# Last stage of a hybrid decoder step: transposes ahead of the values' product, output bank taken later

## The chip, the core and the metric

The kernel runs on one core of a Trainium2 chip, as one launch. Its five engines have their own instruction queues: TensorE (PE; its weight loads, which overlap the products, are shown as PEld), VectorE (DVE), ScalarE (ACT), GpSimd (POOL) and SyncE (SP), which here issues the DMA transfers. The metric is the device time in microseconds (us) of one execution; each version is run several times and the median is compared.

## The reference

One inference step of a two-layer decoder for a prompt (512 positions) and 8 short samples (4 positions each). The first layer is a Mamba-2 mixer, the second a dilated-window attention mixer over a shared K/V. Cut to the second layer, which the change is about:

```
def dilated_mixer(h, attend, biases, g_norm, w_in, w_out):
    u = rmsnorm(h, g_norm) @ w_in
    q = u[..., :Q_WIDTH]  # 3 dilation groups x 8 heads x 128
    gate = u[..., Q_WIDTH:]
    for g in range(3):
        o, lse = attend(q[:, :, g], biases[g], DILATIONS[g], WINDOWS[g] // DILATIONS[g])
    w = softmax(stack(lses)); o = sum(w * outs)
    y = o * silu(gate)
    return y @ w_out
# attend: scores = q k^T * scale + bias, masked to the window; p = softmax(scores); o = p v
```

For the prompt the keys are the 512 positions themselves; for the samples they are 640 kept rows of a cache and the 4 new rows. The final RMSNorm follows.

## The kernel before

All matmuls are in fp32; the large projections are split into a high and a low part (names `whi`, `wlo`, `yh`, `yl`) and are written as three products for each 128-row block. Everything up to the shared K/V lies ahead of the last stage, which runs from about 600 us to the end and which alone the change touches.

The last stage does two things at once. A **filler** (`pair_filler`, L1118, and then `out_proj`, L1421) yields one matmul of a projection at a time: first the query and gate projections by pairs of tiles (outputs `pa` and `pb`, from `bq` and `whi`/`wlo`), then the output projection (from `yh`/`yl` and `wo`). The **attention units** are generators that stop between their parts:

- `attend(h, n)` (L1241): one head h and one block n of 128 prompt queries. Part 1 computes the scores (`sp`, L1254 to L1258: eight products with 32 columns of weights each, one for each quarter of the queries and each of two dilation groups, then one with 128) and the exponentials. Part 2 transposes the weights of the softmax (`ptp`, L1272 to L1276: two or three transposes against the identity) and copies them to `pt`. Part 3 is the values' product (`pv`, L1281 to L1287): first one or two products with the full 128x128 weights, then four with 32 columns and w = 32(n + 1) rows of weights (32, 64, 96 or 128 for n = 0 to 3); ScalarE scales it to `on`. Part 4 transposes `on` into the head's output bank `op` (L1291) and, after the fourth block, copies it out.
- `sample(h, q)` (L1307): one head and four samples. Part 1 loads the cached keys (`kc`, two transfers of 640 KB, L1316), computes the scores (`s`, with 32 columns of weights, L1318 to L1322) and asks for the cached values (`vc`, two transfers, L1337). Part 2 asks for the new values (`vn`, L1340) and transposes (`w`, six transposes). Part 3 is the values' product (`so`, L1350 to L1357): 20 products with 128 rows and 32 columns of weights, then four with 4 rows and 32 columns.

`units` (L1483) puts the units in a row: for each of heads 0 to 6 attend 0, sample 0, attend 1, attend 2, sample 1, attend 3; then for head 7 sample 0, attend 2, sample 1, attend 3, `combine`, attend 0, attend 1. The loop at L1492 goes through them step by step. In step u it advances the units u - 4 (its output transpose), u - 3 (its values' product) and u - 2 (its transposes), in this order, then starts unit u (its scores), and then takes 24 matmuls (20 from step 44 on) from the filler. So each unit is spread over five steps, and TensorE's instructions stand in program order. `kc` and `vc` have two buffers each, both of which one sample unit uses: a unit's `kc` can only be loaded when the scores of the sample unit before have been computed, and its `vc` when that unit's `so` is done. All of these transfers are issued by SP, one after the other in the order in which they stand there.

PSUM has eight banks: three for the projections and five (`pss`, L160) for everything in the attention, so that `op`, `sp`, `ptp`, `pv`, `s1`, `s2`, `w1`, `w2` and `so` share five. The head's `op` is taken by its first unit at the very start of part 1, four steps before its first output transpose.

A scheduler that works with estimated times orders the instructions of ACT, DVE and SP as they come out of the program, so a shift of work can also change their order.

Of the kernel before, what the change touches and what calls it, by code (L numbers as in the profile page):

```python
# [124 lines left out]
def tile_yoco_step(  # L125
# [10 lines left out]
    def pin(ins):  # L136
        if pinned[0]:
            tc.keep_in_program_order(ins)
# [3 lines left out]
    def mm(*a, **k):  # L142
        pin(nc.tensor.matmul(*a, **k))  # L143

    def transpose(*a):
        pin(nc.tensor.transpose(*a))  # L146
# [13 lines left out]
    def pss(name, shape=(128, 512)):  # L160
        return psum.tile(list(shape), F32, name=name, tag="ss", bufs=5)
# [616 lines left out]
    def run(n):  # L778
        for _ in range(n):
            if next(fill, 0) == 0:  # L780
                return
# [275 lines left out]
    qp_t, kv_t = {}, {}  # L1057

    def fetch_kv(h):
        kv_t[h] = kv = half("kv")  # L1060
        dma(kv[:, 0, :], kvd[h, :, 0:T])
        dma(kv[:, 1, 0:SEQ], kvd[h, :, T:T + SEQ])
        for n in range(4):
            dma(kv[32 * n:32 * n + 32, 2, 0:SEQ].rearrange("p (r d) -> p r d", r=4),
                dap(kvd, h * 128 * (T + SEQ) + T + 128 * n, [[T + SEQ, 32], [32 * (T + SEQ), 4], [1, 128]]))
# [153 lines left out]
    def y_split(h, c0, c1):  # L1219
        i, k = h // 4, h % 4  # L1220
        if y_h[i] is None:
            late_split.append((h, c0, c1))
            return
        split2(y_h[i][:, k, c0:c1], y_l[i][:, k, c0:c1], y_t[i][:, k, c0:c1])
# [7 lines left out]
    def bias_tile(h):  # L1232
        bt = wk.tile([128, 512], F32, name="bt", bufs=2)
        for r in range(4):
            dma(bt[32 * r:32 * r + 32, 0:256].rearrange("p (a c) -> p a c", c=32),
                dap(bvd, h * 32 * VN + r * 8 * 63 + 31, [[VN - 1, 32], [63, 8], [1, 32]]))
            dma(bt[32 * r:32 * r + 32, 256:512].rearrange("p (a c) -> p a c", a=2),
                dap(bvd, h * 32 * VN + V0N + 31, [[VN - 1, 32], [V1N, 2], [1, 128]]))
        return bt

    def attend(h, n):  # L1241
        if h not in op_t:
            op_t[h] = pss("op")
        op, bt, qp = op_t[h], bt_t[h], [qp_t[h, g] for g in range(3)]
        kv = kv_t[h]
        kt = kv[:, 0, :]
        vb, vr = (kv[:, i, 0:SEQ].rearrange("p (n d) -> p n d", n=4) for i in (1, 2))
        ktr = kt[:, 0:SEQ].rearrange("p (n r i) -> p r n i", n=4, r=4)
        bt12 = bt[:, 256:512].rearrange("p (a c) -> p a c", a=2)
        w = 32 * (n + 1)  # L1250
        g0 = 128 if n == 0 else 256
        sp = pss("sp")
        k0 = max(0, n - 1) * 128
        for g in range(2):  # L1254
            for r in range(4):
                mm(sp[32 * r:32 * r + 32, g0 + w * g:g0 + w * g + w],
                   qp[1 + g][:, 128 * n + 32 * r:128 * n + 32 * r + 32], ktr[:, r, 0:n + 1, :], start=True, stop=True)
        mm(sp[:, 0:g0], qp[0][:, 128 * n:128 * n + 128], kt[:, k0:128 * n + 128], start=True, stop=True)  # L1258
        s_ = wk.tile([128, 512], F32, name="s", bufs=3)
        mx = wk.tile([128, 4], F32, name="mx", bufs=4)  # L1260
        s12 = s_[:, g0:g0 + 2 * w].rearrange("p (a c) -> p a c", a=2)
        nc.vector.tensor_tensor_reduce(out=s12, in0=sp[:, g0:g0 + 2 * w].rearrange("p (a c) -> p a c", a=2),
                                       in1=bt12[:, :, 128 - w:128], scale=1.0, scalar=-3e38,
                                       op0=ALU.add, op1=ALU.max, accum_out=mx[:, 1:2])
        nc.vector.tensor_tensor_reduce(out=s_[:, 0:g0], in0=sp[:, 0:g0], in1=bt[:, 256 - g0:256], scale=1.0,
                                       scalar=-3e38, op0=ALU.add, op1=ALU.max, accum_out=mx[:, 0:1])
        nc.vector.tensor_scalar(mx[:, 2:3], mx[:, 0:1], mx[:, 1:2], -1.0, op0=ALU.max, op1=ALU.mult)
        nc.scalar.activation(s_[:, 0:g0 + 2 * w], s_[:, 0:g0 + 2 * w], AF.Exp, bias=mx[:, 2:3], accum_out=mx[:, 3:4])
        nc.vector.tensor_tensor(s12[:, 0, :], s12[:, 0, :], s12[:, 1, :], op=ALU.add)
        nc.vector.reciprocal(mx[:, 3:4], mx[:, 3:4])  # L1270
        yield
        tp = pss("ptp", (128, 3, 128))  # L1272
        nk = g0 // 128
        for i in range(nk):
            transpose(tp[:, i, :], s_[:, 128 * i:128 * i + 128], ident)
        transpose(tp[0:w, 2, :], s_[:, g0:g0 + w], ident)  # L1276
        pt = wk.tile([128, 3, 128], F32, name="pt", bufs=2)
        nc.scalar.copy(pt[:, 0:nk, :], tp[:, 0:nk, :])
        nc.scalar.copy(pt[0:w, 2, :], tp[0:w, 2, :])
        yield  # L1280
        pv = pss("pv")[:, 0:128]  # L1281
        for i in range(nk):
            b = n - nk + 1 + i
            mm(pv, pt[:, i, :], vb[:, b, :], start=i == 0, stop=False, skip_group_check=True)
        for r in range(4):
            mm(pv[32 * r:32 * r + 32, :], pt[0:w, 2, 32 * r:32 * r + 32], vr[0:w, r, :],
               start=False, stop=True, skip_group_check=True)  # L1287
        on = wk.tile([128, 128], F32, name="on", bufs=1)
        nc.scalar.activation(on, pv, AF.Copy, scale=mx[:, 3:4])
        yield  # L1290
        transpose(op[:, 128 * n:128 * n + 128], on, ident)  # L1291
        op_n[h] = op_n.get(h, 0) + 1
        yt = y_t[h // 4][:, h % 4, :]
        if h == 7 and op_n[h] % 2 == 0:
            c0 = HA if n > 1 else 0
            assert len(gated) == 2
            nc.vector.scalar_tensor_tensor(yt[:, c0:c0 + HA], op[:, c0:c0 + HA], 0.5, yt[:, c0:c0 + HA], op0=ALU.mult, op1=ALU.mult)
            y_split(h, c0, c0 + HA)
        elif h < 7 and op_n[h] == 4:
            nc.vector.tensor_copy(yt[:, 0:SEQ], op)  # L1300
            att_done.add(h)
# [107 lines left out]
    op_t, op_n, bt_t, late_smp = {}, {}, {}, []  # L1409
# [66 lines left out]
    def run(n):  # L1476
        m = min(n, ahead[0]) if n > OCN else 0
        ahead[0] -= m
        for _ in range(n - m):
            if next(fill, 0) == 0:  # L1480
                return

    units = [(f, (h, i)) for h in range(ATH - 1) for f, i in  # L1483
             ((attend, 0), (sample, 0), (attend, 1), (attend, 2), (sample, 1), (attend, 3))]
    units += [(sample, (7, 0)), (attend, (7, 2)), (sample, (7, 1)), (attend, (7, 3)), (combine, ()), (attend, (7, 0)), (attend, (7, 1))]
    fill = filler()
    fetch_kv(0)
# [4 lines left out]
    for u in range(len(units) + LA + 2):  # L1492
        i = u - LA
        if u == len(units) - 3 + SKIP:
            ahead[0] = ATH * OCN
        for j in (i - 2, i - 1, i):
            if 0 <= j < len(units):
                next(live[j], 0)
        if u < len(units):
            f, a = units[u]  # L1500
            if f is attend and a[0] not in bt_t:
                bt_t[a[0]] = bias_tile(a[0])
            if f is attend and a[1] == 2 and 0 < a[0] < ATH - 1:
                fetch_kv(a[0] + 1)
            live.append(f(*a))
            next(live[u])
        run(FILL[u >= SLOW])
# [97 lines left out]
```

## Time and profile before

| what | us |
|---|---|
| median of 3 runs (lowest, highest) | 964.43 (963.14, 966.48) |
| the profiled execution, device time | 964.79 |
| its span, from the first to the last instruction | 963.0 |
| TensorE busy (share of the span) | 932.9 (97%) |
| VectorE busy | 682.2 (71%) |
| ScalarE busy | 482.1 (50%) |

The device time is 1.8 us longer than the span that the trace shows. A matmul's record lasts longer than the time by which it holds up the next, since matmuls overlap; so what a group of them costs is read from the start of its first record to the start of the next group's first record, not from busy time. In the rows, a shape such as 128\*32 is rows times columns of the weights, and 128x272 that of the moving operand. One fp32 matmul leaves two records, a transpose one.

### The profile page before, as it was taken

How to read it: one execution, taken by the hardware profiler on the slowest of the kernel's cores; microseconds unless marked ns; L12 is line 12 of the kernel's file. 1: busy time of each engine (PE TensorE's matmuls, PEld its weight loads, DVE VectorE, ACT ScalarE, POOL GpSimd, SP SyncE). 2: the span in 40 equal slices, each digit the busy share in tenths (PEclk: the TensorE clock that was granted, in tenths of full speed). 3: DMA queues.
4: the chain of work that ended last, by engine and by line, in shares of the span. 5: the costliest groups of instructions: out<-in, count | busy, mean ns of one | idle time of the engine just before them, and what ended most of it. 6: DMA issues, size and time to landing. Idle time of an engine off the chain costs nothing.

```text
span 963.0 us, 21807 instructions
## 1 busy us (share of the span) xinstructions
PE 932.9 (97%) x8645; PEld 847.5 (88%) x8645; DVE 682.2 (71%) x1435; ACT 482.1 (50%) x1057; POOL 200.5 (21%) x295
## 2 busy tenths in 40 slices
PE   7999998999999998999999999999999999989996
PEld 5999987889788888999999999888888888868896
DVE  6687979998998798555597347767667766757532
ACT  5558745654645654322354214555555555555542
POOL 3232545544544532111010000000000000000021
PEclk9999999899999999999999999999999999989898
DMA  7252355255366432545386556775876876844411
GB/s 259 83 157 74 120 201 190 78 166 180 130 194 205 160 114 95 154 139 194 117 272 188 197 180 188 257 251 181 271 234 197 266 264 208 276 163 158 143 45 50
DMA packets 75934, 168.49 MB, mean 175 GB/s; under 512 B 19446, under 2 KB 37192, under 8 KB 75320
## 3 DMA queue, kind: packets, MB, share of 16 engines
q1 hardware_dynamic: 71880, 154.91, 49.0%
q10 hardware_dynamic: 2880, 9.44, 2.5%
q0 software_dynamic: 1072, 2.74, 1.1%
q8 instruction: 68, 1.11, 0.5%
q14 instruction: 34, 0.28, 0.1%
HBM read 141.14 MB, written 25.93 MB: 173 GB/s over the span
## 4 chain that ended last, share of the span: by engine, by line
PE 88%; DVE 5%; DMA 3%; ACT 1%; POOL 1%; issue 1%; DVEq 0%; SPq 0%; ACTq 0%
PE pa L143 34%; PE pb L143 30%; PE sp L143 3%; PE so L143 3%; PE pv L143 2%; PE s L143 2%; PE yd L143 1%; PE ptp L146 1%; PE w L146 1%; PE csp L143 1%; PE yo L143 1%; DMA m<-aed 1%; PE xp L146 1%; DMA kc<-ck 1%; PE yos L143 1%; DVE vl L758 1%
## 5 line engine op out<-in xcount | busy, mean ns | idle before, releaser
L199 ACT ACTIVATE whi<-wraw 128x1024 fp32r<-128x1024 f32 x72 | 76.2, 1058 | 99.6 <-PE pb L143 66.2
L200 DVE TENSOR_TENSOR wlo<-wraw,whi 128x1024 fp32r<-128x1024 f32 x71 | 88.9, 1252 | 50.5 <-ACT whi L199 50.5
L143 PE MATMUL pa<-bq,whi 128*128 128x272 f32 x512 | 103.1, 297 | 0.0
L143 PE MATMUL pa<-xh,whi 128*128 128x256 f32 (+1 forms) x320 | 92.7, 293 | 3.3 <-ACT xh L365 3.3
L143 PE MATMUL pb<-xh,whi 128*128 128x288 f32 (+1 forms) x304 | 90.4, 299 | 3.9 <-ACT cb L331 3.9
L143 PE MATMUL pb<-xl,whi 128*128 128x288 f32 (+1 forms) x304 | 91.2, 302 | 0.9 <-DVE xl L368 0.8
L143 PE MATMUL pa<-xl,whi 128*128 128x256 f32 (+1 forms) x320 | 90.8, 287 | 0.9 <-DVE xl L368 0.8
L143 PE MATMUL pb<-xh,wlo 128*128 128x288 f32 (+1 forms) x304 | 87.4, 299 | 0.0
L143 PE MATMUL pa<-xh,wlo 128*128 128x256 f32 (+1 forms) x320 | 85.0, 283 | 0.0
L143 PEld LDWEIGHTS pa<-bq,whi 128*128 128x128 f32 x512 | 81.9, 190 | 0.9
L143 PE MATMUL pb<-bq,whi 128*128 128x272 f32 x384 | 79.9, 302 | 0.3 <-DVE kv L1100 0.2
L143 PE MATMUL pa<-bq,wlo 128*128 128x272 f32 x256 | 74.2, 290 | 0.0
L529 DVE SCALAR_TENSOR_TENSOR co<-cb,cvp,co 128x568 f32<-128x568 f32 x72 | 66.6, 925 | 1.2 <-ACT co L527 0.2
L143 PEld LDWEIGHTS pa<-xh,whi 128*128 128x128 f32 x320 | 60.7, 190 | 6.2 <-ACT xh L365 3.7
L143 PEld LDWEIGHTS pb<-bq,whi 128*128 128x128 f32 x384 | 62.5, 194 | 1.7 <-DVE qpad L1091 0.7
L143 PEld LDWEIGHTS pa<-xl,whi 128*128 128x128 f32 x320 | 60.6, 189 | 3.4 <-DVE xl L368 1.4
L143 PEld LDWEIGHTS pb<-xl,whi 128*128 128x128 f32 x304 | 57.8, 190 | 6.5 <-issue 4.4
L143 PEld LDWEIGHTS pb<-xh,whi 128*128 128x128 f32 x304 | 58.0, 191 | 5.0 <-ACT cb L331 4.1
L1332 POOL COPY lse<-mxs 128x1 f32<-128x1 f32 x16 | 3.8, 236 | 273.3 <-DVE mxs L1330 273.3
L143 PEld LDWEIGHTS pa<-xh,wlo 128*128 128x128 f32 x320 | 58.0, 188 | 1.3 <-issue 0.9
L1158 ACT ACTIVATE whi<-wraw 128x512 fp32r<-128x512 f32 x64 | 40.2, 628 | 37.4 <-PE pa L143 17.1
L143 PEld LDWEIGHTS pb<-xh,wlo 128*128 128x128 f32 x304 | 56.6, 190 | 2.2 <-issue 2.2
(378 smaller groups left out, 2786.8 us busy)
## 6 DMA issues: line engine op xcount, KB each, us to landing
wraw<-w_in SPq DMA_DIRECT2D x40, 512.0 KB
kc<-ck SPq DMA_DIRECT2D x32, 640.0 KB
vc<-cv SPq DMA_DIRECT2D x32, 640.0 KB
wraw<-wb SPq DMA_DIRECT2D x32, 512.0 KB
s<-s SPq DMA_DIRECT2D x16, 512.0 KB
m<-aed SPq DMA_DIRECT2D x16, 512.0 KB
ssmS<-s ACTq DMA_DIRECT2D x16, 512.0 KB
wraw<-w_out SPq DMA_DIRECT2D x16, 512.0 KB
```

The source lines that it names most:

```text
L143: pin(nc.tensor.matmul(*a, **k))
L146: pin(nc.tensor.transpose(*a))
L199: a = nc.scalar.activation(hi, raw, AF.Copy)
L200: b = lo_eng.tensor_tensor(lo, raw, f32(hi), op=ALU.subtract)
L529: nc.vector.scalar_tensor_tensor(o, cb[:, k:k + n], cvp[:, ti, k:k + 1], o, op0=ALU.mult, op1=ALU.add)
L758: nc.vector.scalar_tensor_tensor(v_l[g][:, i, :], v_t[g][:, i, :], gg, f32(v_h[g][:, i, :]), op0=ALU.mult, op1=ALU.subtract)
L1158: nc.scalar.activation(hi, src[p][j], AF.Copy)
L1332: nc.gpsimd.tensor_copy(lse[:, i16:i16 + 1], mx[:, 2:3])
```

## The change

Two edits. The loop now advances unit u - 4, then u - 2, then u - 3: within a step the transposes (`ptp` or `w`) stand right behind the output transpose and ahead of the values' product (`pv` or `so`), which now stands right ahead of the new unit's scores. And a head takes its output bank `op` when its first output transpose is issued, four steps later than before.

```
@@ attend
     def attend(h, n):
-        if h not in op_t:
-            op_t[h] = pss("op")
-        op, bt, qp = op_t[h], bt_t[h], [qp_t[h, g] for g in range(3)]
+        bt, qp = bt_t[h], [qp_t[h, g] for g in range(3)]
...
         on = wk.tile([128, 128], F32, name="on", bufs=1)
         nc.scalar.activation(on, pv, AF.Copy, scale=mx[:, 3:4])
         yield
+        if h not in op_t:
+            op_t[h] = pss("op")
+        op = op_t[h]
         transpose(op[:, 128 * n:128 * n + 128], on, ident)
...
@@ the loop over the units
-        for j in (i - 2, i - 1, i):
+        for j in (i - 2, i, i - 1):
             if 0 <= j < len(units):
                 next(live[j], 0)
```

On TensorE, in a step that starts an attend unit (`sp`) and advances an attend unit's product (`pv`) and a sample unit's transposes (`w`), the difference is:

```order
 L146 MATMUL op<-ident,on 128x128
+L146 MATMUL w_7710<-ident,ss 128x128 x4
+L146 MATMUL w_7711<-ident,ss 128x128
+L146 MATMUL w_7711<-ident,ss 4x128
 L143 MATMUL pv<-kv,pt 128x128 x2
 L143 MATMUL pv<-kv,pt 32x128 x4
-L146 MATMUL w_7719<-ident,ss 128x128 x4
-L146 MATMUL w_7720<-ident,ss 128x128
-L146 MATMUL w_7720<-ident,ss 4x128
 L143 MATMUL sp<-kv,qp 32x32 x8
```

The six transposes now follow the output transpose and precede the values' product, which borders on the scores. In the next step, with a sample unit's product, it is the same with `ptp` and `so`:

```order
 L146 MATMUL op<-ident,on 128x128
+L146 MATMUL ptp<-ident,s 128x128 x3
 L143 MATMUL so<-vc,wt 32x128 x20
 L143 MATMUL so<-vn,wt 32x128 x4
-L146 MATMUL ptp<-ident,s 128x128 x3
```

The three transposes moved from behind the product to ahead of it. On SP the order of the transfers stays as it was, but for three places; the one that lies between steps 42 and 44 (sample units of head 7, `kc` and `vc` of the text above; `wraw` are weights of the filler) stood before as

```order
L1237 DMA bt_10908<-bvd_92 32x2x128
L190 DMA wraw_10937<-wb 128x1024
L1337 DMA vc_10832<-cv 128x1280
L1337 DMA vc_10834<-cv 128x1280
L1340 DMA vn_10979<-vnd_97 4x4x128
L1316 DMA kc_10995<-ck 128x1280
L1316 DMA kc_10997<-ck 128x1280
```

and stands now (its lines are one higher there) as

```order
L1237 DMA bt_10908<-bvd_92 32x2x128
L190 DMA wraw_10936<-wb 128x1024
L1317 DMA kc_10994<-ck 128x1280
L1338 DMA vc_10832<-cv 128x1280
L1338 DMA vc_10834<-cv 128x1280
L1341 DMA vn_10969<-vnd_97 4x4x128
L1317 DMA kc_10996<-ck 128x1280
```

The first of the two `kc` transfers for the sample unit of step 44 moved ahead of the `vc` transfers of the unit before; the second stayed behind them. The other two places are early ones, where a bias transfer and a weight transfer pass ahead of a `vc`. In the last steps the transposes of attend 0 of head 7 (`ptp`) move ahead of the products of `combine` (`oc`), and ACT and DVE take the two casts of the output weights (L199, L200) some instructions earlier.

## Rows read from the trace of the kernel before

**Rows 1.** The first lines of the profile's page: the span, and busy time, share of the span and instructions of each engine.

```profile
span 963.0 us, 21807 instructions
PE 932.9 (97%) x8645; PEld 847.5 (88%) x8645; DVE 682.2 (71%) x1435; ACT 482.1 (50%) x1057; POOL 200.5 (21%) x295
```

**Rows 2.** Busy time by stretches of 10 us in the last stage: stretch, its length, busy time and instructions of PE, PEld, DVE, ACT, POOL, then the granted TensorE clock (1.00 is 2.4 GHz, 0.50 is 1.2 GHz), the share of the DMA engines' time, GB/s.

```profile
700.00:710.00 10.00, 10.00 (x136) 8.68 (x135) 6.44 (x20) 5.96 (x15) 0.00 (x0) 1.00 0.64 204
...
860.00:870.00 10.00, 9.69 (x109) 7.68 (x110) 3.83 (x13) 4.39 (x9) 0.18 (x1) 0.67 0.12 17
```

**Rows 3.** Who waited for whom, PE's matmuls alone, from 600 us to the end: total, times, longest.

```profile
PE s L143 <- DMA kc<-ck: 2.6, 2, 2.2
PE pa L143 <- ACT yh L1214: 2.3, 1, 2.3
```

**Rows 4.** Timeline of PE in a step with `op`, `pv`, `w` and `sp`: start, duration to the end of the last of the row's records, engine, line, what, number of records. The last row is the filler's first matmul.

```profile
702.33 0.27 PE L146 MATMUL op<-ident,on 128*128 128x128 f32 x1
702.44 0.97 PE L143 MATMUL pv<-kv,pt 128*128 128x128 f32 x12
703.34 0.87 PE L146 MATMUL w<-ident,ss 128*128 128x128 f32 x6
704.14 0.75 PE L143 MATMUL sp<-kv,qp 128*32 128x32 f32 x18
704.65 0.49 PE L143 MATMUL pb<-bq,whi 128*128 128x272 f32 x2
```

**Rows 5.** The same for the next step, with `op`, `so`, `ptp` and `s`, and its filler's first matmul.

```profile
707.73 0.27 PE L146 MATMUL op<-ident,on 128*128 128x128 f32 x1
707.93 1.30 PE L143 MATMUL so<-vc,wt 128*32 128x128 f32 x40
709.16 0.42 PE L143 MATMUL so<-vn,wt 4*32 4x128 f32 x8
709.51 0.55 PE L146 MATMUL ptp<-ident,s 128*128 128x128 f32 x3
709.99 1.28 PE L143 MATMUL s<-kc,qpad 128*32 128x512 f32 x16
711.24 0.52 PE L143 MATMUL pa<-bq,whi 128*128 128x272 f32 x2
```

**Rows 6.** The same in step 46, where the transposes `w` are followed by another full-width transpose (`lp`, of `combine`).

```profile
873.74 0.87 PE L146 MATMUL w<-ident,ss 128*128 128x128 f32 x6
874.45 0.27 PE L146 MATMUL lp<-ident,lse 128*16 128x128 f32 x1
```

**Rows 7.** Who waited for whom, PE's weight loads alone, 602 to 850 us: total, times, longest ("issue": no releaser is seen).

```profile
PEld ptp L146 <- issue: 3.4, 17, 0.2
...
PEld w L146 <- issue: 2.8, 14, 0.2
PEld ptp L146 <- PE so L143: 1.8, 9, 0.2
...
PEld s L143 <- DMA kc<-ck: 0.4, 1, 0.4
```

**Rows 8.** Timeline of SP: start, duration of the issue, what (x2: two transfers). The last of them is followed in time by Rows 9.

```profile
656.47 0.83 SPq L1337 DMA_DIRECT2D vc<-cv  x2
...
667.69 0.83 SPq L1316 DMA_DIRECT2D kc<-ck  x2
...
844.61 0.37 SPq L190 DMA_DIRECT2D wraw<-wb  x1
850.10 0.83 SPq L1337 DMA_DIRECT2D vc<-cv  x2
...
851.36 1.01 SPq L1316 DMA_DIRECT2D kc<-ck  x2
```

**Rows 9.** The chain of waits that ended last: start, length, what.

```profile
851.73 8.54 DMA kc<-ck
```

**Rows 10.** As Rows 2, stretches of 1 us (the last two numbers are the DMA engines' share and GB/s).

```profile
672.00:673.00 1.00, 1.00 (x19) 0.82 (x21) 0.95 (x5) 0.48 (x1) 0.00 (x0) 1.00 0.66 267
673.00:674.00 1.00, 1.00 (x40) 0.80 (x36) 0.96 (x4) 0.15 (x1) 0.00 (x0) 1.00 0.04 15
...
850.00:851.00 1.00, 1.00 (x23) 0.63 (x23) 0.00 (x1) 0.43 (x2) 0.00 (x0) 1.00 0.00 0
```

**Rows 11.** Timeline of PE: the scores `s` that the `kc` of Rows 8 belong to (674.71), and those of steps 42 and 44 with the waits in brackets, the filler's first matmul behind step 42 (845.47) and step 44 (862.64), and the first of step 45 (866.99).

```profile
674.71 1.28 PE L143 MATMUL s<-kc,qpad 128*32 128x512 f32 x16
...
843.66 1.62 PE L143 MATMUL s<-kc,qpad 128*32 128x512 f32 x12
...
845.47 0.52 PE L143 MATMUL pa<-bq,whi 128*128 128x272 f32 x2
...
855.74 0.88 PE L146 MATMUL w<-ident,ss 128*128 128x128 f32 x6
858.82 1.10 PE L143 MATMUL s<-kc,qpad 128*32 128x512 f32 x4 [2.20 <-DMA kc<-ck]
860.31 1.06 PE L143 MATMUL s<-kc,qpad 128*32 128x512 f32 x6 [0.40 <-DMA kc<-ck]
...
862.64 0.82 PE L143 MATMUL pb<-bq,whi 128*128 128x272 f32 x2
...
866.99 0.27 PE L146 MATMUL op<-ident,on 128*128 128x128 f32 x1
```

More of the change, by code (lines that the diff above doesn't have):

```diff
@@ L1241, in attend @@
     def attend(h, n):
-        if h not in op_t:
-            op_t[h] = pss("op")
-        op, bt, qp = op_t[h], bt_t[h], [qp_t[h, g] for g in range(3)]
+        bt, qp = bt_t[h], [qp_t[h, g] for g in range(3)]
         kv = kv_t[h]
@@ L1290, in attend @@
         yield
+        if h not in op_t:
+            op_t[h] = pss("op")
+        op = op_t[h]
         transpose(op[:, 128 * n:128 * n + 128], on, ident)
@@ L1495, in tile_yoco_step @@
             ahead[0] = ATH * OCN
-        for j in (i - 2, i - 1, i):
+        for j in (i - 2, i, i - 1):
             if 0 <= j < len(units):
```

## Prediction

> **What bounds the kernel now.** The page's head comes first: TensorE is busy for 932.9 of 963.0 us, 97%, the next engine for 71% [rows 1]. That is an average, so the second view is busy time by stretches in the stage that changes: in 700 to 710 us PE is busy for 10.00 of 10.00 us at the full granted clock, and DMA has a share of 0.64 [rows 2]. The third is who waits for whom: of PE's matmuls behind 600 us two wait for cached keys (2.6 us in all) and one in the tail for `yh` (2.3 us); there is none for a PSUM bank, for `pt`, `wt` or `on` [rows 3]. So up to step 43 the stage is exactly as long as PE's instruction stream, and a change of order can save only what the order itself costs inside that stream. That is read from the timeline, from start to start.
>
> **What a change of shape costs.** An `op` transpose holds up the full-width `pv` behind it by 0.11 us (702.33 to 702.44) [rows 4], but the 32-column `so` by 0.20 (707.73 to 707.93) [rows 5]: leaving the full width costs 0.09. A second pair agrees: six `w` transposes take 0.80 until `sp` starts [rows 4], 0.71 until the full-width `lp` does [rows 6], again 0.09. Entering the full width costs as well: 0.71 for six transposes is 0.06 more than 6 x 0.11, and three `ptp` take 0.48 until `s` (709.51 to 709.99) [rows 5], which is 3 x 0.11 + 0.09 + 0.06. Narrow products before them end late, too: the four 4-row `so` take 0.35 (709.16 to 709.51), where 20 with 128 rows take 1.23, 0.0615 each [rows 5]; 0.35 less 4 x 0.0615 leaves 0.10. So a narrow shape that borders on another shape pays 0.09 to 0.10, and the entry 0.06.
>
> The weight loads show the same places: between 602 and 850 us, 17 + 14 + 9 = 40 loads of `ptp` and `w` wait for 0.2 us each, 8.0 in all, nearly one a step [rows 7].
>
> **The order of transposes and product.** A step before runs full (filler, `op`), narrow product, full (`ptp` or `w`), narrow scores, full (filler). After, the transposes lie in the first full run and the product borders on the scores. Gone are the product's exit into the transposes (0.10), the entry (0.06) and the transposes' exit into the scores (0.09): 0.25. Added is the border of product and scores. Where shapes differ (4 rows after `so`, 32 or 64 rows in `pv` of n = 0 and 1, against 128 rows) I price it as the exit between narrow and other, 0.10. Where `pv` ends with 96 or 128 rows (n = 2, 3) I take none. Bounds: 0.10 there as well, which gives back 1.3; and nothing at any border, which gains 2.8 more. I take the middle because the 4-row border is in the trace and costs, while 20 equal `so` run on without one [rows 5].
>
> The Trainium skill, page "TensorEngine Tiling (Array Packing)", Key Properties, states that changing the tiling mode, not just the tile, drains TensorE, and lists row modes of 128, 64 and 32. By that list 96 rows have no mode of their own, as I take it; were they one, the saving would be 0.7 us less. No row here shows a 96-row product beside scores.
>
> So a step saves 0.15. It has all its parts from step 3 to step 43, 41 steps: 41 x 0.15 = 6.15. Thirteen of them advance a `pv` of n = 2 or 3 (two for each of heads 0 to 6, less the last): 13 x 0.10 = 1.3. Sum 7.45 by the end of step 43. An upper bound for the 0.15 is the weight loads' whole wait of 0.2 a step, 8.2 in all; the lower is 0.09 a step, if the 0.06 was only the wait of the first transpose for its input, 3.7.
>
> **The output bank.** Nothing. PE waits for no bank [rows 3], so a bank that is taken four steps later frees nothing that anyone waits for. The last user of the bank that `op` now gets is a group of an earlier step, and the filler's 24 matmuls (704.65 to 707.73, 3.08 us) [rows 4, 5] cover its eviction. Bounds: 0 to +0.3, if an `op` transpose had to wait for the head before to be copied out, seven times at 0.04.
>
> **The transfers.** A `vc` is asked for behind a `so`, the next `kc` behind an `s`, and the scores come a fixed number of steps later. With shorter steps that distance shrinks while the transfers don't. One such path before: `vc` issued at 656.47, `kc` at 667.69 [rows 8], `s` at 674.71 [rows 11], 18.24 us. The last traffic ends soon after 672.7 (share 0.66 in 672 to 673, 0.04 in the next) [rows 10], so at most some 2 us were left, less what passes between the last packet and the signal that the matmul waits for, which no row shows. After, `so` borders on the scores, so `vc` is asked for 0.48 later within its step (the `ptp` ahead of it), and three steps are 0.55 shorter in all: 17.2. That uses up half of the margin or more; I take no new wait, and bound it by 0.1 to 0.5 at each of the dozen sample steps (third rival).
>
> Step 42 waited already: `s` to filler takes 1.81 (843.66 to 845.47) [rows 11] against 1.25 (709.99 to 711.24) [rows 5], 0.56, and its weight load 0.4 for `kc` [rows 7]. Its `kc` hangs on the scores of step 40, so what two steps save, 0.4, turns into wait there. Cover gone: 0.4 lost.
>
> **Step 44** is the one that ends late. Before, `vc` was issued at 850.10 and `kc` behind it at 851.36 [rows 8], though its buffers were free since step 42 and DMA stood at 0.00 in 850 to 851 [rows 10]: SP issues in order, and `vc` waited for `so`. The chain shows one `kc` from 851.73 on for 8.54 us [rows 9], and PE waited 2.20 and 0.40 [rows 11]. Four transfers in 8.6 us are 2.15 each. Now one `kc` goes ahead of `vc`, into the idle stretch; three are left, and the last lands 2.15 earlier, counted from `vc`. `vc` itself is asked for 0.3 later within the step (`ptp` ahead of `so`, 0.48, less the 0.15 and rounding). Steps up to there have brought 7.45 - 0.15 - 0.4 = 6.9. So the scores of step 44 go on 6.9 + 2.15 - 0.3 = 8.75 earlier. PE reaches them 6.9 to 7.05 earlier and would still wait some 2 us: the wait keeps its size but in one piece. Behind it the granted clock was 0.67 in 860 to 870 [rows 2], and I leave that as it was. Bounds of this step: 0.9 less if the three go at the 267 GB/s of a busy stretch [rows 10] (3 x 655,360 bytes in 7.4 us against 6.45), and 2.9 more if the clock stays up (second rival).
>
> Steps 45 to 48 save four times 0.14, 0.55. In the tail the products of `combine` and the casts change places around the wait of 2.3 for `yh` [rows 3]; nothing by my count, with bounds of -2.3 and +2.3, since no row says what else would come last.
>
> **Sum.** 8.75 + 0.55 = 9.3. The span goes from 963.0 to 953.7 [rows 1]; with the 1.8 outside the span 955.5. The profiled execution, at 964.79, lies 0.36 above the median of 964.43; less that, 955.1, rounded to 955.0.
>
> **Rivals.**
> 1. *Forecast*, 955.0, with its own range of 953.5 to 957.5 by the bounds of the border price and of the three transfers.
> 2. *The clock stays up at step 44.* The filler there took 4.35 for 20 matmuls (862.64 to 866.99) [rows 11]; at the pace of 3.08 for 24 it is 2.57, so 1.8 less; the rest of the scores took 2.33 (860.31 to 862.64), against 1.25 for a whole one [rows 5], 1.1 less. Together 2.9: 952. For it: the wait of one `kc` is gone. Against: the other is still waited for by some 2 us, about as long as the one that stood ahead of the fall.
> 3. *The scores catch up with the keys.* Without margin, a dozen sample steps wait 0.3 to 0.6 each, 3.6 to 5 us given back: 958 to 960. For it: 0.56 in step 42. Against: step 42 is the only one with a wait up to 850 us [rows 7].
> 4. *It doesn't do what it says.* The cost belongs to every border of groups, not to a change of shape; the same number of groups then costs the same and only step 44's transfer helps, 2.15 less 0.3: 962.6, no difference. Against: 0.11 and 0.20 behind the same `op` [rows 4, 5].
> 5. *Slower.* The scores catch up with the keys so far that PE stands as in step 44, 2.2 of wait and then 2.9 at the half clock, 5.1 a time. The place is `s` of the sample units of heads 1 to 6. Two such waits eat the 9.3, and from there it is slower; with three it is 955.1 + 15.3 = 970.4. It needs a `kc` that lands over 2 us later than I count. For it: 64% DMA share in a common stretch [rows 2]. Against: the margin loses 1.04 of about 2.
>
> **Chances.** Forecast 0.58, clock up 0.24, scores catch up 0.07, nothing done 0.05, slower 0.05, and 0.01 for the tail at its upper bound. The range reaches from 950.5 (second rival with the border free, in part) to 960.0. A measurement of this kernel tells about 0.3%, 2.9 us, from no change. The first three cases are faster by more, the fourth is within it, the fifth is slower: 0.90, 0.05, 0.05.
>
> **What would show it.** The wait of the weight loads of `w` and `ptp` gone; `op` to `w` or `ptp` 0.11; `so` to `s` about 0.10 longer than its products; step 42 waiting about 1.0 and no other sample step before it; one `kc` of step 44 in time and the other landing some 1.5 to 2 us behind PE; the filler behind it at 4.35 (forecast) or 2.6 (second rival). Wrong it would be above all if `kc` waits show in rows of steps before 42, or if `pv` ahead of the scores costs more than the transposes did.

## The result, and the profile after

The changed kernel takes 955.47 us (median of 4 runs, 954.65 to 958.56), beside 964.04 for the kernel before (4 runs, 963.14 to 966.48; the three known at the time of the prediction had a median of 964.43). The ratio is 0.9913, with a 95% interval of 0.9884 to 0.9942: faster by 0.9%. The profiled execution took 955.35, its span is 953.6 us. Forecast were 955.0 and a span of 953.7. The sum came out almost to the tenth, but not all of its terms did. Left out of the medians below are two executions in a slower state, one of e3 (1014.85 us at a granted clock of 0.84) and one of e7 (1465.11 us at 0.56).

The head of the profile's page of the changed kernel (beside [rows 1]):

```profile
span 953.6 us, 21793 instructions
PE 924.2 (97%) x8645; PEld 850.3 (89%) x8645; DVE 685.5 (72%) x1435; ACT 477.6 (50%) x1057; POOL 201.9 (21%) x295
```

TensorE (PE) has the same number of records, 8645, and the same share of the span. What changed is how much one group of them holds up the next. The timeline of PE in the same two steps as in [rows 4, 5], from the output transpose to the filler's first matmul, and ahead of them two rows of a step that advances an n = 0 block (32 rows of weights):

```profile
683.71 0.74 PE L143 MATMUL pv<-kv,pt 128*128 128x128 f32 x10
684.38 1.17 PE L143 MATMUL sp<-kv,qp 128*32 128x96 f32 x18
...
700.62 0.27 PE L146 MATMUL op<-ident,on 128*128 128x128 f32 x1
700.72 0.82 PE L146 MATMUL w<-ident,ss 128*128 128x128 f32 x6
701.38 0.96 PE L143 MATMUL pv<-kv,pt 128*128 128x128 f32 x12
702.16 0.73 PE L143 MATMUL sp<-kv,qp 128*32 128x32 f32 x18
702.64 0.49 PE L143 MATMUL pb<-bq,whi 128*128 128x272 f32 x2
...
705.74 0.27 PE L146 MATMUL op<-ident,on 128*128 128x128 f32 x1
705.85 0.49 PE L146 MATMUL ptp<-ident,s 128*128 128x128 f32 x3
706.27 1.30 PE L143 MATMUL so<-vc,wt 128*32 128x128 f32 x40
707.50 0.42 PE L143 MATMUL so<-vn,wt 4*32 4x128 f32 x8
707.85 1.28 PE L143 MATMUL s<-kc,qpad 128*32 128x512 f32 x16
...
709.10 0.39 PE L143 MATMUL pa<-bq,whi 128*128 128x272 f32 x1
```

From the first record of the step to the filler's first: with `w` and `pv` 2.02 us (700.62 to 702.64), before 2.32 [rows 4]; with `ptp` and `so` 3.36 (705.74 to 709.10), before 3.51 [rows 5]. The six `w` now hold up what follows them by 0.66 (0.80 before), the three `ptp` by 0.42 (0.48). `pv` of step 18 is of n = 2, with 96 rows of weights: it runs into `sp` after 0.78, where before it took 0.90 until `w`. For n = 0 nothing of that kind shows: 0.67 from `pv` to `sp` (683.71 to 684.38), as it took 0.67 to `w` before in the same step (684.33 to 685.00), so this border still costs, as forecast.

The weight loads that waited 0.2 us in nearly every step [rows 7] show the same. Who waited for whom, PE's weight loads alone, 602 to 848 us of the changed kernel (total in us, times, longest):

```profile
PEld s L143 <- issue: 5.8, 21, 0.3
...
PEld sp L143 <- issue: 4.6, 23, 0.2
...
PEld s L143 <- DMA kc<-ck: 1.8, 2, 1.1
```

No `ptp` and no `w` waits in this answer any more; the waits that are left are those in front of `s`, `sp` and `so`, one or two a step, and one for `kc`, of 1.8 us in two places, where it was 0.4 in one [rows 7]. These places, and step 44, in PE's timeline (beside [rows 11]):

```profile
672.83 1.53 PE L143 MATMUL s<-kc,qpad 128*32 128x512 f32 x10
...
674.97 0.52 PE L143 MATMUL pa<-bq,whi 128*128 128x272 f32 x2
...
837.07 1.80 PE L143 MATMUL s<-kc,qpad 128*32 128x512 f32 x10
...
839.48 0.52 PE L143 MATMUL pa<-bq,whi 128*128 128x272 f32 x2
...
848.71 0.82 PE L146 MATMUL w<-ident,ss 128*128 128x128 f32 x6
...
853.06 0.62 PE L143 MATMUL s<-kc,qpad 128*32 128x512 f32 x6 [1.89 <-DMA kc<-ck]
...
854.30 0.52 PE L143 MATMUL pb<-bq,whi 128*128 128x272 f32 x2
...
856.91 0.27 PE L146 MATMUL op<-ident,on 128*128 128x128 f32 x1
```

A whole `s` takes 1.25. In step 13 it takes 2.14 (672.83 to 674.97), so 0.89 of wait that was not there before [rows 11]; in step 42 it takes 2.41, so 1.16 of wait (0.56 before). In step 44 the last keys come at 853.06, 7.25 earlier than before, and the filler behind takes 2.61 for its 20 matmuls (854.30 to 856.91) instead of 4.35 [rows 11]. SP's timeline of the transfers behind these waits (beside [rows 8]):

```profile
667.22 0.83 SPq L1317 DMA_DIRECT2D kc<-ck  x2
...
839.40 0.35 SPq L1317 DMA_DIRECT2D kc<-ck  x1
844.44 0.80 SPq L1338 DMA_DIRECT2D vc<-cv  x2
...
845.97 0.33 SPq L1317 DMA_DIRECT2D kc<-ck  x1
```

The keys of step 13 are asked for only 0.47 earlier than before (667.22, 667.69 [rows 8]), while their scores come 1.88 earlier (672.83, 674.71). The first keys of step 44 are asked for at 839.40, as the scores of step 42 end, the others at 845.97 behind `vc`: one ahead, one behind, as the order showed.

The ledger of the two profiles, from step 4 on (at 620.06 in both), with what was forecast:

| term, us | forecast | measured |
|---|---|---|
| PE's stream of steps 4 to 43, waits for `kc` taken off | -7.3 | -7.63 (234.23 to 226.60) |
| new wait in step 13 | 0 to 0.1 | +0.89 |
| longer wait in step 42 | +0.4 | +0.60 |
| step 44 up to the last keys (`w` or `pv` to the second `s` row) | -1.85 | -1.11 |
| half clock behind it: rest of the scores, filler | 0 | -2.83 |
| steps 45 to 48 | -0.55 | -0.28 |
| tail from step 49 on | 0 | +0.96 |
| sum | -9.3 | -9.4 |

The forecast of the stream is 7.45 less the 0.15 of step 3. Of the 0.33 more, most comes from the steps whose `pv` has 96 or 128 rows: the one shown above saves 0.30, and 0.25 was forecast. Steps 45 to 48 save less than forecast, in part because in steps 46 and 48 a further full-width transpose (`lp`) stands among the groups; these two save 0.04 each. The rest of the scores took 2.33 before (860.31 to 862.64) and 1.24 now; with the filler that is 1.09 + 1.74 = 2.83.

### The profile page after: what moved, and what is told of

Its sections match the earlier page's. It is cut to its first block, busy times and chain, and to the rows that moved or that the text cites. A ratio compares the mean times of both kernels' runs of the same rounds, so it can differ in the third digit from the quotient of the medians.

```text
span 953.6 us, 21793 instructions
## 1 busy us (share of the span) xinstructions
PE 924.2 (97%) x8645; PEld 850.3 (89%) x8645; DVE 685.5 (72%) x1435; ACT 477.6 (50%) x1057; POOL 201.9 (21%) x295
## 3 DMA queue, kind: packets, MB, share of 16 engines
q8 instruction: 68, 1.11, 0.5%
## 4 chain that ended last, share of the span: by engine, by line
PE 87%; DVE 6%; DMA 3%; ACT 1%; POOL 1%; issue 1%; SPq 0%; DVEq 0%; ACTq 0%
PE pa L143 34%; PE pb L143 30%; PE sp L143 3%; PE so L143 3%; PE pv L143 2%; PE s L143 2%; DMA kc<-ck 1%; PE yd L143 1%; PE csp L143 1%; PE yo L143 1%; PE ptp L146 1%; PE xp L146 1%; PE w L146 1%; DVE co L529 1%; PE yos L143 1%
## 5 line engine op out<-in xcount | busy, mean ns | idle before, releaser
L199 ACT ACTIVATE whi<-wraw 128x1024 fp32r<-128x1024 f32 x72 | 76.1, 1056 | 101.5 <-PE pb L143 68.9
L200 DVE TENSOR_TENSOR wlo<-wraw,whi 128x1024 fp32r<-128x1024 f32 x71 | 90.0, 1268 | 48.1 <-ACT whi L199 47.9
```

The source lines that it names most:

```text
L199: a = nc.scalar.activation(hi, raw, AF.Copy)
L200: b = lo_eng.tensor_tensor(lo, raw, f32(hi), op=ALU.subtract)
```

## Experiments

Each ratio is to runs of the kernel before on the same chip. "Stream" is, for each, the time from step 4 to step 44 less the waits of `s` for `kc` in it, read from the starts of PE's records. Stream, waits and step 44 are those of the one execution that has a profile; it took 961.60 in e7, the longest of nine, 951.67 in e9, the longest of five, and 953.30 in e8, the shortest of five, so these do not add up to the medians.

| run | edit | median, us | ratio to before (95%) | stream | waits for `kc`, steps 13 to 42 | step 44 |
|---|---|---|---|---|---|---|
| before | | 964.04 | | 234.23 | 0.56 | 7.80 |
| after | both | 955.47 | 0.9913 (0.9884 to 0.9942) | 226.60 | 2.05 | 5.59 |
| e1_order_only | order alone | 954.71 | 0.9911 (0.9891 to 0.9931) | 226.57 | 4.44 | 6.49 |
| e2_bank_only | bank alone | 964.02 | 1.0007 (0.9994 to 1.002) | 234.22 | 0.84 | 7.54 |
| e3_product_first | third order | 963.89 | 1.0008 (0.9987 to 1.0029) | 233.94 | 0 | 8.51 |
| e5_after_keys44_pool | after, keys of 44 by GpSimd | 952.32 | 0.9889 (0.985 to 0.9929) | 226.52 | 3.33 | 2.66 |
| e6_before_keys44_pool | before, the same | 957.31 | 0.994 (0.9917 to 0.9964) | 234.24 | 0.19 | 2.95 |
| e7_after_keys44_late | after, keys of 44 behind values | 957.17 | 0.9944 (0.9924 to 0.9963) | 226.74 | 4.28 | 9.20 |
| e8_new_values_first | after, `so` reordered | 955.76 | 0.993 (0.9904 to 0.9955) | 224.68 | 2.06 | 9.13 |
| e9_keys7_pool_new_first | e8, keys of head 7 by GpSimd | 949.03 | 0.9854 (0.9831 to 0.9878) | 224.65 | 2.71 | 2.66 |

(Step 44 is from its first record to the filler's first.)

**e1_order_only and e2_bank_only.** The two edits, each alone: in e1 the changed line of the loop with `op` taken as before, in e2 the reverse.

```
-        for j in (i - 2, i - 1, i):
+        for j in (i - 2, i, i - 1):
```

> Only the order of the loop (output transpose, transposes, product, scores); the bank is taken early as before. Theory (what is saved is changes of weight-tile shape on TensorE): all of the gain, 955 to 956, step for step the times of the changed kernel (3.36 us for a step with op, ptp, so and s, 2.03 for one with op, w, pv of three or four blocks and sp). Rival (the later bank has a share): 958 to 962, with waits for a bank in front of the scores.

> Only the bank is taken later; the order is that of before. Theory: nothing, 963.5 to 965, steps as before (3.51 and 2.31 us). Rival (the bank has a share): 958 to 962.

The order has all of the gain, the bank none. Both also show a known order a second time: e2 issues the same instructions in the same order as the kernel before on every engine, and e1 the same as the changed kernel; only the banks differ. So what differs between e2 and before, or e1 and after, does not come from the order. The streams agree within 0.03 us. The clock behind step 44 does not: in e2 the filler there runs at full speed, in e1 not quite. PE's timeline of e2, and then of e1:

```profile
861.23 2.56 PE L143 MATMUL s<-kc,qpad 128*32 128x512 f32 x10 [2.23 <-DMA kc<-ck]
...
864.78 0.52 PE L143 MATMUL pb<-bq,whi 128*128 128x272 f32 x2
...
867.39 0.27 PE L146 MATMUL op<-ident,on 128*128 128x128 f32 x1
```

```profile
856.93 0.81 PE L143 MATMUL s<-kc,qpad 128*32 128x512 f32 x6 [1.95 <-DMA kc<-ck]
...
859.01 0.82 PE L143 MATMUL pb<-bq,whi 128*128 128x272 f32 x2
...
862.35 0.27 PE L146 MATMUL op<-ident,on 128*128 128x128 f32 x1
```

The filler of step 44 takes 2.61 in e2 (864.78 to 867.39) where the same instructions took 4.35 before, and 3.34 in e1 (859.01 to 862.35) where they took 2.61 after. A wait of 1.95 is followed by the half clock in e1, one of 1.89 is not in the changed kernel.

**e3_product_first.** A third order; the number of groups in a step is the same.

```
-        for j in (i - 2, i, i - 1):
+        for j in (i - 1, i - 2, i):
```

> A third order with as many groups in a step: product first, then output transpose and transposes in one row, then scores (bank taken late). The narrow product stands between two full-width runs, as before. Theory of shapes: a step costs what it cost before (3.51 us with so, 2.31 with pv of n = 2 or 3), 962 to 965 in all. Rival (the gain comes from output transpose and transposes standing in one row, or from fewer waits of the transposes for their inputs): 3.36 and 2.1 us, 955 to 957.

PE's timeline in the two steps, and then who waited, weight loads alone, 602 to 850 us:

```profile
704.23 0.96 PE L143 MATMUL pv<-kv,pt 128*128 128x128 f32 x12
705.12 0.33 PE L146 MATMUL op<-ident,on 128*128 128x128 f32 x1
705.28 0.82 PE L146 MATMUL w<-ident,ss 128*128 128x128 f32 x6
```

```profile
PEld op L146 <- issue: 3.8, 19, 0.2
```

Here `op` and `w` stand in one row, as in the changed kernel, but a narrow product stands between them and the filler. Now `op` pays the entry: it holds up `w` by 0.16 (705.12 to 705.28) instead of 0.11, and its weight load is the one that waits. The stream is back at 233.94, 0.29 below that of before, and the time is that of before. So the gain is not in having output transpose and transposes side by side; it goes with how many times a step leaves and enters the full width.

**e8_new_values_first.** In `so` the four products with 4 rows of weights go first; start and stop flags move with them.

```
-        for i in range(6):
+        for i in (5, 0, 1, 2, 3, 4):
...
```

> The changed kernel, with the four products of the new values (4 rows of weights) ahead of the 20 of the cached ones (128 rows) in so, so that so ends with the shape with which s begins. The same instructions, one change of shape fewer in a step. Theory (a change of rows costs 0.10 wherever it stands): op to s takes 2.0 us instead of 2.11 in every so step (step 3.25 instead of 3.36), 1.5 to 1.8 us in all 16 of them: 953 to 954.5. Rival (only full against narrow costs): 3.36 as it is, 955.

```profile
705.19 0.27 PE L146 MATMUL op<-ident,on 128*128 128x128 f32 x1
...
705.72 0.42 PE L143 MATMUL so<-vn,wt 4*32 4x128 f32 x8
706.07 1.30 PE L143 MATMUL so<-vc,wt 128*32 128x128 f32 x40
707.19 1.26 PE L143 MATMUL s<-kc,qpad 128*32 128x512 f32 x16
...
708.41 0.52 PE L143 MATMUL pa<-bq,whi 128*128 128x272 f32 x2
```

PE's timeline in a `so` step: 3.22 us (705.19 to 708.41) instead of 3.36, 0.14 less for one change of shape less, and the stream is 1.92 shorter. The 20 cached products hold up what follows by 1.12 (706.07 to 707.19) where they took 1.23 in front of the 4-row ones (706.27 to 707.50 above): a change of rows between narrow products costs 0.11, near the 0.10 that I took, and `s` itself ends a little sooner without it. The median did not follow. In the profile SP's order came out with both keys of step 44 behind `vc` (`vc` at 843.00, `kc` at 844.27 and 844.64), and that step took 9.13 instead of 5.59.

**e5_after_keys44_pool, e6_before_keys44_pool, e7_after_keys44_late.** The place of step 44's keys, in both orders.

```
-            dma(kc[jp], ck[h, q, :, 2 * jp:2 * jp + 2, :])
+            (nc.gpsimd.dma_start if (h, q) == (7, 1) else dma)(kc[jp], ck[h, q, :, 2 * jp:2 * jp + 2, :])
```

In e7 the `kc` and `vc` transfers of head 7 are held in program order on SP instead.

> The changed kernel, with both key transfers of step 44 issued by GpSimd, so that they don't stand behind the values in SP's queue. Theory (the keys' place in the queue is a term of its own, and what is left of it is the 1.9 to 2.9 us that PE waits in step 44): no wait there, scores of step 44 in 1.25 us instead of 4.2, 951.5 to 954. Rival (the keys land late because of the DMA engines, not of the queue): wait stays, 955.

> The kernel before with the same: both key transfers of step 44 issued by GpSimd. Theory (the order itself saves 7 to 8 us by shapes; the transfer is worth the wait of 2.6 and, if the half clock behind it was the wait's doing, 2.8 more): 958 to 961, steps 3 to 43 unchanged at 3.51 and 2.31 us. Rival (the gain of the change was mostly the transfer that moved ahead): 955 to 957.

> The changed kernel with the values' and keys' transfers of head 7 held in program order, so that both keys of step 44 stand behind the values, as before the change. Theory (one transfer ahead is worth one transfer time): the last keys land 2 to 2.6 us later, PE waits 4 to 4.5 us in step 44, 957 to 958; and if a longer wait there brings the half clock back (filler of step 44 at 4.2 instead of 2.5 us), 960. Rival (no matter what is ahead): 955.

With the keys out of SP's queue step 44 has no wait in either order (2.66 and 2.95). The stream doesn't move. e6 is 6.3 us faster than before by medians taken on one chip (963.60 to 957.31), e5 5.0 faster than e6: with the place of the keys equal, the order is worth 5.0; in the profiles its stream is 7.7 shorter, and 3.1 more of waits in steps 13, 37 and 42 go off that. In e7 PE waits 3.87 for the keys and step 44 takes 9.20, 3.6 more than after; the median, 957.17, is the forecast one. From the end of that wait the scores take 3.72 (granted clock 0.57 in 859 to 863 us), the filler behind them 2.61. So in this execution the half clock came with the longer wait, but in the scores and not in the filler, for which 960 was forecast. That the wait brought it is not shown.

**e4_after_keys_early.** In the changed kernel every sample unit asks for the next unit's keys as soon as its own scores are written.

```
+        if i16 < 15:
+            kc_load((i16 + 1) // 2, (i16 + 1) % 2)
         vc = []
...
```

> The changed kernel, with the keys of the next sample unit asked for as soon as a unit's scores are written, three steps earlier in the program. Theory (what the change leaves unused are waits for keys: 0.89 us in step 13, 1.16 in step 42, 1.89 in step 44): all three go, 951 to 952. Rival (the transfers are limited by the DMA engines, so the waits move to the values or to other steps): 954 to 957.

This expectation failed: 973.32, ratio 1.0112 (1.0087 to 1.0137), slower than before. The waits for `kc` are gone, and others came. PE's waits from 600 to 900 us:

```profile
PE ptp L146 <- ACT s L1266: 7.2, 3, 4.8
PE w L146 <- ACT ss L1339: 6.8, 2, 3.8
```

The transposes of five steps wait for their exponentials, since the scheduler, with transfers at other times, put work for the filler ahead of the scores' maxima on DVE: in one case the maximum of scores that were complete at 708.43 was taken at 716.32, right behind a weight's split (`wlo`) that had begun at 715.71.

```profile
716.32 0.68 DVE L1334 CUSTOM_DVE_ANT_0 ss<-s,sbt 128x512 f32<-128x512 f32 x1
```

So it says nothing against the keys; it says that moving transfers here can move DVE's order too. (In e6 one instruction of DVE has another place than before, in e5 some twenty have another than after, all from step 44 on.)

**e9_keys7_pool_new_first.** e8 with all keys of head 7 issued by GpSimd.

> The changed kernel with two things together: the four new-value products first in so, and all key transfers of head 7 (steps 42 and 44) issued by GpSimd. Theory (TensorE's own stream and the waits for keys are separate terms that add up): stream of steps 4 to 43 at 224.7 us as with the first alone, no wait in steps 42 and 44 (1.0 to 2.4 and 1.9 to 6 before), the waits of 0.7 to 1.4 in step 13 left: 946 to 950. Rival (the DMA engines are full there, so the keys land late from any queue): 952 to 955, with waits in 42 or 44.

949.03, 1.5% faster than the kernel before and the fastest here. Step 44 has no wait, but step 42 still has one of 1.66: the theory's "no wait in step 42" fell there, and the rival is right for that step. Busy time in one stretch, columns as in [rows 2], shortly before the scores of step 42 (at 838.63):

```profile
833.00:836.00 3.00, 3.00 (x38) 2.75 (x35) 2.34 (x10) 1.31 (x5) 0.00 (x0) 1.00 1.00 352
```

The DMA engines have a share of 1.00. GpSimd asked for these keys at 828.96 and 830.94, right behind the values that SP had asked for from 827.62 on; the second of them took 9.3 us to land, that of step 44 (asked for at 843.54) 6.1. Stream and step 44 add up as expected.

## Why the prediction was right, and where it was not

**The shapes: right.** The stream of steps 4 to 43 is 7.63 shorter, 7.3 forecast, and hardly varies between runs of one order (234.22 to 234.24, 226.52 to 226.74). e1 and e2 give it to the order, e3 and e8 to the changes of shape: one taken away saves 0.14, and a third order with as many as before costs as before. The fourth rival, that the cost belongs to every border of groups, is out. The middle price held: a border of unlike narrow shapes costs 0.11 (0.10 forecast), that of `pv` with 96 or 128 rows costs nothing. The Trainium skill, page "TensorEngine Tiling (Array Packing)", Tiling Modes, lists row modes of 128, 64 and 32 and none of 96. That a 96-row product then counts as one of 128 the page does not say; the rows of step 18 agree with it: 0.78 from `pv` to `sp`, 0.12 less than before. One price of the prediction is a little off: 0.71 for six transposes is 0.05, not 0.06, more than 6 x 0.11.

**The bank: right.** Nothing, within 0.2% (e2). The 0.04 a head in its upper bound stands in no row.

**Step 44's keys: right in kind, mis-sized.** The step that failed is "the last lands 2.15 earlier, counted from `vc`". Counted so it is 1.59 (7.25 less the 5.66 by which `vc` was issued earlier), inside the bound that the prediction gave for it. `vc` was asked for 0.32 later within its step, as forecast.

**The margin of the keys: this step failed.** "That uses up half of the margin or more; I take no new wait" holds for all sample steps but some of the first ones of a head. In step 13 PE waits 0.89, in e1 1.37, and step 19 waits 1.17 in e1 and 1.47 in e7, none in the others. The shortening was forecast well: from the issue of `vc` (655.64, the one at 656.47 in [rows 8]) to the scores it is now 17.19, and 17.2 was forecast. What was mis-sized is the margin. From the issue of these keys to their scores it was 7.02 before (667.69 to 674.71) and is 5.61 now (667.22 to 672.83); of these 1.41, 0.89 came back as a wait, so by this estimate, if the keys take as long to land in both, some 0.5 had been left, and not about 2. The keys of a head's first sample unit also stand in SP's queue behind the head's twelve bias transfers, which did not get faster with the steps: 9.23 from the first of them to the keys before (658.46 to 667.69), 9.27 now (657.95 to 667.22). SP's waits ahead of two of them, 655 to 669 us, of the kernel before and then of the changed one (total in us, times, longest):

```profile
SPq L1235 <- DMA wraw<-wb: 2.7, 1, 2.7
SPq L1237 <- DMA vc<-cv: 1.2, 1, 1.2
```

```profile
SPq L1237 <- DMA vc<-cv: 2.3, 1, 2.3
SPq L1235 <- DMA wraw<-wb: 1.1, 1, 1.1
```

By the profile these bias transfers wait for the values and the weights ahead of them to land, 3.9 us in all before and 3.4 now; why they do is open. So the keys were asked for 0.47 earlier where their scores came 1.88 earlier. The third rival is partly true: not a dozen steps, but two or three, and 2.1 to 4.4 us in all against 0 to 0.8 in the old order. (Its own sum was off: a dozen waits of 0.3 to 0.6 are 3.6 to 7.2, not 3.6 to 5.) It is the term that the change leaves behind.

**The half clock: this step failed.** "Behind it the granted clock was 0.67, and I leave that as it was." This clock is not set by the order of the instructions. Stretches of 10 us, columns as in [rows 2], of the kernel before, of e2, and of the changed kernel and e1 in the tail:

```profile
890.00:900.00 10.00, 7.60 (x50) 6.74 (x51) 7.21 (x19) 6.47 (x17) 0.00 (x0) 0.83 0.57 205
900.00:910.00 10.00, 10.00 (x73) 9.44 (x73) 3.95 (x5) 4.06 (x6) 0.00 (x0) 0.83 0.12 29
```

```profile
860.00:870.00 10.00, 8.77 (x108) 6.02 (x112) 3.80 (x13) 5.78 (x15) 0.18 (x1) 0.83 0.27 89
```

```profile
880.00:890.00 10.00, 7.54 (x47) 6.95 (x47) 7.24 (x18) 4.98 (x14) 0.00 (x0) 0.70 0.52 182
890.00:900.00 10.00, 10.00 (x70) 9.57 (x69) 3.00 (x5) 4.06 (x6) 0.00 (x0) 0.78 0.05 6
```

```profile
880.00:890.00 10.00, 9.58 (x85) 9.08 (x83) 6.34 (x16) 4.74 (x12) 0.00 (x0) 1.00 0.86 316
890.00:900.00 10.00, 7.67 (x63) 7.16 (x64) 5.21 (x14) 5.18 (x13) 0.00 (x0) 1.00 0.18 55
```

In 860 to 870 us, around the end of step 44, it was 0.67 before [rows 2] and 0.83 in e2, with the same instructions in the same order. In the tail (from the output transpose of step 49 to the last one) before takes 21.96 us, after 22.88, e1 18.86; the clock kept back in these stretches, 10 us times what the granted clock lacks of 1.00, summed, is 3.4, 5.2 and 0 us. So the changed kernel's profile won 2.83 at step 44, which is the second rival's 2.9, and lost 0.96 in the tail, where the clock was lower and the order had changed too; how much is due to which is open, but e1, in the changed kernel's order, took 4.02 less at the full clock. The terms that were missed nearly cancel: -2.83 + 0.96 + 0.89 + 0.74 (keys of step 44) + 0.27 (steps 45 to 48) + 0.20 (step 42) is +0.2, and the stream was 0.33 better than forecast. That the total is right to half a microsecond is therefore luck: its largest term, the stream, was right, and the errors of the others happened to cancel.

**What stays open.** When the half clock comes in a given run is not shown. Nor is what the medians owe to it, since only one execution of each kernel has a profile.

## What to carry to other kernels

Write down the shape of the weights along TensorE's stream, and count the borders where it changes; a step that runs full, narrow, full, narrow can be put in an order with one pair less, which saved 0.15 to 0.30 us a step here (fp32). Products inside one group may be sorted for it too (0.14 for moving four of 24). When a stage gets faster, look at each transfer whose distance to its user is counted in steps, and at what stands ahead of it in its queue: here 1.5 to 4 us of 7.6 went back there, and the place of two transfers was worth 3 to 6 more.

A term that rests on the granted clock in one profile is a range, not a number.

## What was not expected of the hardware

The granted clock of the same instructions differed from run to run: the filler of step 44 took 4.35 us in one profile of an instruction order and 2.61 in another, 2.61 and 3.34 in the two of the other order, with waits of 1.9 to 2.2 us ahead of it in all four (and a second one of 0.4 in the kernel before). And the DMA engines, at a share of 0.64 in a common stretch of 10 us [rows 2], were at 1.00 in 833 to 836 us ahead of step 42 in e9, and a queue of their own did not bring the keys in time there.
